# Attention probabilities transposed by VectorE blocks and SBUF-to-SBUF transfers instead of by TensorE

## Chip, core and metric

One core of a Trainium2 chip runs the whole program. The metric is the device time of one execution in microseconds (us); lower is better. Engines: PE is TensorE (PEld its weight loads), DVE VectorE, ACT ScalarE, POOL GpSimd, and SP issues all transfers here.

## What is computed

One layer of a generator over 1024 latent and 256 context tokens, width 1024, in float32. All tokens are normalised and projected; two branches follow, a gated linear attention (GLA) and a differential attention; gates merge them, and an output projection and a residual end the layer. The change lies in the differential attention: 8 heads, each with two sets of queries and keys of width 64 and one set of values of width 128.

```python
def diff_attention(q1, q2, k1, k2, v, lam):        # lq = 1024, keys = 1280
    def one_block(qs):                             # 128 queries
        qb1, qb2 = qs
        s1 = einsum('bhqd,bhkd->bhqk', qb1, k1) * scale
        s2 = einsum('bhqd,bhkd->bhqk', qb2, k2) * scale
        a = softmax(s1) - lam * softmax(s2)
        return einsum('bhqk,bhkv->bhqv', a, v)

o_diff = diff_attention(...)
b = merge_heads(rms_norm(o_diff) * diff_gain * (1 - lam_init)) * silu(diff_gate)
y = sigmoid(m_gla) * (a @ w_br_gla) + sigmoid(m_diff) * (b @ w_br_diff)
x = x + g_x * (y @ w_out)                          # g_x: a vector of the conditioning
```

## The kernel before

Full precision on PE is had by splitting: a float32 value becomes a rounded part `hi` and the difference `lo`, and a product is three matmuls (`mm3`: hi*hi, hi*lo, lo*hi). So whatever goes into such a product first needs a rounding and a subtraction.

The program runs in phases that overlap: projections (`phase_a`), GLA heads, differential attention with "filling" projections between its matmuls (`phase_b`, `fill`), and the branch and output projections (`phase_c`).

What sets the order of the work is a planner, class `Driver`. Each piece of the program is a Python generator that issues instructions and yields points in a planned time. The driver keeps a planned time for each engine, for the issue of transfers and for the tiles, by fixed costs, and resumes the generator with the best priority that is due. The result is one fixed order of instructions for each engine; on the chip each engine executes its own list in order and waits on semaphores. Buffers are counted: `acq(tag)` waits in the plan for a free buffer of a tag, `rel(tag, e)` gives one back; `TAGS` holds the number of each.

Attention goes over 8 heads and, in each, 8 query tiles `qt` of 128 queries; two tiles make a pair `pr`, so there are 64 tiles and 32 pairs. The steps of a tile:

- `att_scores`: PE writes both score rows (128 x 1280 each) into the PSUM tile `s5` (in profile rows `s`), 8 matmuls of 512 columns and 4 of 256. Queries `aq` and keys `kk` come from DRAM.
- `att_max`, `att_exp`: DVE takes the maxima (`sm<-s`), ACT the exponentials with their sums (`e<-s,sm`) into two `e5` tiles (rows `e`).
- `att_mix`: DVE combines both into one tile, `e<-e,sm,e`, 128 x 1280.
- `att_tr`: PE transposes the ten 128 x 128 blocks through PSUM (`b<-ident,e`; the last tiles `mc<-ident,e`), in groups of 4, 4 and 2 blocks (`GROUPS`).
- `att_split`, `split2`: ACT copies each group out of PSUM (`ac<-b`), POOL rounds it (`at<-ac`) and subtracts (`at<-ac,at`).
- `att_av`: for a pair, PE multiplies with the values, 30 matmuls of 256 columns (`b<-at,vv`).
- `att_fin`: two PE transposes of the result, squares on ACT, POOL's inverse root, a scaling on DVE (`b1k<-b1k,sm`), two PE transposes, a split, and a store to `d_bT`. Gates come from DRAM (`b1k<-d_dg`).

`fill` puts half tiles of other projections (24 matmuls of 512 columns, `mb<-h,wt`) on PE where the plan finds room, paced by `PACE`; its weights are loaded to `raw` and split to `wt` by ACT and DVE. `first_two` starts the product with `w_br_diff`, which needs `d_bT` of all heads back from DRAM (`h<-d_bT`). The gate vector `g_x`, halved, is computed once in `job_gate` as the tile `gb` and used in the last phase.

All engine instructions have the line of a helper: L190 for ACT, DVE and POOL, L326 for matmuls, L352 for PE transposes, L291 for transfers. So rows are read by tile names.

Of the kernel before, what the change touches and what calls it, by code (L numbers as in the profile page):

```python
# [221 lines left out]
class Hybrid:  # L222

    TAGS = dict(
        h0=("sb", 16), h1=("sb", 16), raw=("sb", 3), gb=("sb", 1), sm=("sb", 48), kk=("sbK", 3),
# [3 lines left out]
        hc=("sbA1", 16), g5=("sbA1", 6), l5=("sbA1", 3),  # L229
# [7 lines left out]
        e5=("sbB", 6), at4=("sbB", 6), at2=("sbB", 2), ac=("sbB", 2), b1k=("sbB", 5), fin=(None, 2),  # L237

        ya=("sbC", 8), yb=("sbC", 8), yc=("sbC", 8), yf=("sbC", 16), sf=("sbC", 2), o=("sbC", 4), wr=("sbC", 8),
# [141 lines left out]
    def scratch(self):  # L381
        d = self.dram
        self.d_q = [d(f"d_q{h}", [P, S]) for h in range(4)]
        self.d_k = [d(f"d_k{h}", [P, T]) for h in range(4)]
        self.d_la = [[d(f"d_la{r}{h}", [P, T]) for h in range(4)] for r in range(2)]
        self.d_v = [d(f"d_v{c}", [T, 512]) for c in range(2)]
        self.d_gg = [d(f"d_gg{c}", [S, 512]) for c in range(2)]
        self.d_dg = [d(f"d_dg{c}", [S, 512]) for c in range(2)]
        self.d_dv = [[d(f"d_dv{j}{c}", [T, 512]) for c in range(2)] for j in range(2)]
        self.d_qT = [d(f"d_qT{c}", [4, P, 2, S]) for c in range(2)]  # L390
        self.d_kT = [[d(f"d_kT{j}{c}", [4, P, T]) for c in range(2)] for j in range(2)]
        self.d_aT = [[d(f"d_aT{j}{h}", [2, P, S]) for h in range(4)] for j in range(2)]
        self.d_bT = [[d(f"d_bT{j}{i}", [P, S]) for i in range(8)] for j in range(2)]
        self.d_m = [[d(f"d_m{j}{i}", [P, S]) for i in range(8)] for j in range(2)]
        self.d_y = [d(f"d_y{i}", [P, S]) for i in range(8)]
# [333 lines left out]
    def job_gate(self):  # L729
# [4 lines left out]
        gb = self.gb = self.t("gb", [P, 2, 512])  # L734
        for n in range(2):
# [27 lines left out]
            self.rel("p", self.pool.tensor_scalar(gb[:, n], bias, 0.5, 0.0, ALU.mult, ALU.add))  # L763

# [29 lines left out]
    def phase_a(self):  # L794
# [6 lines left out]
        self.ev_rope = [Event(), Event()]  # L801
        self.ev_gla, self.ev_stream = Event(), Event()
# [57 lines left out]
    def to_gla(self):  # L860
        yield self.ev_la
        yield from self.idle("hc", "g5", "l5", "gs", "go", "gt")
# [638 lines left out]
    def att_mix(self, u):  # L1501
# [6 lines left out]
        if x in self.PC:  # L1508
            self.pool.tensor_scalar(E[1], E[1], cf, 0.0, ALU.mult, ALU.add)
            e = self.pool.tensor_tensor(E[0], E[0], E[1], ALU.add)  # L1510
# [4 lines left out]
        d.set(self.ev_a[u["hd"], u["qt"]], e)  # L1515
# [6 lines left out]
    def att_tr(self):  # L1522

        d = self.d
        for hd in range(8):
            for qt in range(8):
                x = qt % 2
                yield self.ev_a[hd, qt]
                E = self.att[hd, qt][0]
                if x == 0:  # L1530
                    A = self.aT[hd, qt // 2] = []
                for g, (k0, n) in enumerate(self.GROUPS):
                    if x == 0:
                        tg = "at4" if n == 4 else "at2"
                        yield from self.acq(tg, 2)
                        A.append([self.t(tg, [P, n, 2, P], F32R) for _ in range(2)] + [tg])
                    hi, lo = A[g][:2]
                    tb = "mc" if "psC" in self.pools else "b1"
                    yield from self.acq(tb)
                    pt = self.t(tb, [P, n, P])  # L1540
                    for j in range(n):
                        e = self.tr(pt[:, j], E[:, (k0 + j) * P:(k0 + j + 1) * P])
                    d.spawn(self.att_split(g, pt, hi[:, :, x], lo[:, :, x], self.ev_aT[hd, qt, g], tb), On(e, "ACT"), prio=self.PS)
                    yield AtPE(0)
                self.rel("e5", e)

    def att_av(self):
        d = self.d
        for hd in range(8):
            for pr in range(4):  # L1550
                for x in range(2):
                    yield self.ev_aT[hd, 2 * pr + x, 0]
                A = self.aT[hd, pr]
# [5 lines left out]
                for g, (k0, n) in enumerate(self.GROUPS):  # L1559
                    hi, lo, tg = A[g]  # L1560
                    for x in range(2):
                        yield self.ev_aT[hd, 2 * pr + x, g]
                    for j in range(n):
                        kt = k0 + j
                        e = self.mm3(po, VH[:, kt], VL[:, kt], hi[:, j].rearrange("p x t -> p (x t)"),
                                     lo[:, j].rearrange("p x t -> p (x t)"), kt == 0, kt == 9)
                        if j % 2:
                            yield AtPE(0)
                    self.rel(tg, e, 2)
                if pr == 3:  # L1570
                    self.rel("vv", e, 2)
                d.spawn(self.att_fin(hd, pr, po, [self.att[hd, 2 * pr + x][1] for x in range(2)]), On(e, "ACT"), prio=self.PF)
# [12 lines left out]
    def att_split(self, g, pt, hi, lo, ev, tag):  # L1585
        e = yield from self.split2(pt, hi, lo, tag, g in self.SG)
        self.d.set(ev, e)

    def split2(self, pt, hi, lo, tag, pool):

        yield from self.acq("ac")
        c = self.t("ac", [P, 4, P])[:, :pt.shape[1]]
# [13 lines left out]
    def att_fin(self, hd, pr, po, zs):  # L1606
# [7 lines left out]
        e = self.act.activation(ot, po, AF.Copy)  # L1614
# [23 lines left out]
        yield On(self.pool.tensor_tensor(ss, ss, self.nhalf[:, 0:2], ALU.pow), "DVE")  # L1638
        for x in range(2):
            e = self.dve.tensor_scalar(oo[:, x], g[:, x], ss[:, x:x + 1], None, ALU.mult)  # L1640
# [17 lines left out]
    def fill(self):  # L1658
# [17 lines left out]
        def conv(n, raw):  # L1676
# [6 lines left out]
            yield d.on("DVE", hi)  # L1683
            e = self.dve.tensor_tensor(lo, raw, hi.bitcast(F32), ALU.subtract)
# [100 lines left out]
    def first_two(self, evs, ws, rhs):  # L1785
# [3 lines left out]
        yield self.ev_aT[7, 7, 2]  # L1789
# [18 lines left out]
    def phase_b(self):  # L1808
# [22 lines left out]
        self.ev_aT = {(hd, qt, g): Event() for hd in range(8) for qt in range(8) for g in range(3)}  # L1831
        self.aT = {}
# [29 lines left out]
    def phase_c(self):  # L1862
# [6 lines left out]
        def to_c():  # L1869
# [6 lines left out]
            yield from self.idle("b1", "e5", "b1k", "aq", "kk", "vv", "at4", "at2", "ac")  # L1876
# [68 lines left out]
        def right():  # L1945

            w = {}

            def gate(n, k):
                x = w[n, k]  # L1950
                self.dve.tensor_tensor(x, x, self.gb[:, int(n[2]) - 1], ALU.mult)
# [148 lines left out]
```

## Time and profile before

| | before |
|---|---|
| three runs | 1717.92, 1720.37, 1720.63 us |
| median | 1720.37 us |
| span of the profiled execution, first to last instruction | 1714.5 us |
| busy PE, DVE, ACT, POOL | 1674.2, 1057.7, 738.3, 728.8 us |
| share of 16 DMA engines, moved | 48%, 258.8 MB |

The execution that was profiled has no time of its own besides its span; the span stands 5.9 us below the median of the runs. A profile row of a group reads: line, engine, operation, out<-in, shape, count | busy us, mean ns of one | idle us just before them, and what ended it. A row of the timeline reads: start us, us taken, engine, line, operation, tiles, count. The three numbers of a wait are us in total, times, and the longest.

### The profile page before, as it was taken

To read this page: it belongs to the slowest core of one execution; us is meant where nothing else is said; L and a number is where in the kernel's file an instruction comes from. 1 tells how busy PE (TensorE), PEld (TensorE's weight loads), DVE (VectorE), ACT (ScalarE), POOL (GpSimd) and SP (SyncE) were. 2 spreads that over 40 slices of the span, in tenths; PEclk is the share of its full clock that TensorE was granted. 3 is DMA by queue.
4 is the path that set the end of the run, shared out by engine and by line. 5 is a ranking of instruction groups with operands and counts; after the bars stand their busy time and mean duration, and the time that the engine had idled before them with its cause. 6 is when DMAs were issued, how large, how long until landed. Compare 5 with 4: busy or idle time off the path is not lost.

```text
span 1714.5 us, 24744 instructions
## 1 busy us (share of the span) xinstructions
PE 1674.2 (98%) x8557; PEld 1389.4 (81%) x8557; DVE 1057.7 (62%) x1933; ACT 738.3 (43%) x1509; POOL 728.8 (43%) x917
## 2 busy tenths in 40 slices
PE   8899999999999999999999989999999999999999
PEld 3788788888888888888888878888888888887887
DVE  4534325615564767767763788777877778325694
ACT  4636522212242443344342566656656556311231
POOL 1500002403324445444541577878878778710000
PEclk9999999999999999999999999999999999999999
DMA  8523344453743544535444244435436753269421
GB/s 309 158 86 122 143 154 149 140 171 115 221 163 114 202 142 147 168 125 168 160 129 143 91 119 137 117 108 145 133 105 185 226 156 114 84 238 333 148 98 74
DMA packets 244748, 258.81 MB, mean 151 GB/s; under 512 B 20840, under 2 KB 176400, under 8 KB 244624
## 3 DMA queue, kind: packets, MB, share of 16 engines
q1 hardware_dynamic: 244624, 257.25, 47.7%
q8 instruction: 67, 1.10, 0.3%
q14 instruction: 57, 0.47, 0.1%
HBM read 170.68 MB, written 86.51 MB: 150 GB/s over the span
## 4 chain that ended last, share of the span: by engine, by line
PE 87%; POOL 4%; DVE 2%; DMA 2%; ACT 2%; issue 2%; SPq 0%; ACTq 0%; DVEq 0%; POOLq 0%
PE mm L326 42%; PE mc L326 11%; PE mb L326 8%; PE s L326 7%; PE b L326 5%; POOL at L190 4%; PE b L352 3%; PE go L326 3%; PE gs L326 2%; PE gt L326 2%; PE tp L352 2%; DVE sm L190 1%; PE mz L326 1%; DMA w<-in_w_ada 1%; PE gt L352 1%
## 5 line engine op out<-in xcount | busy, mean ns | idle before, releaser
L326 PE MATMUL mm<-w,h 128*128 128x512 f32 x2304 | 569.3, 399 | 1.5 <-DVE w L190 1.5
L326 PEld LDWEIGHTS mm<-w,h 128*128 128x128 f32 x2304 | 425.6, 188 | 87.6 <-DVE w L190 2.1
L190 POOL TENSOR_TENSOR at<-ac,at 128x512 fp32r<-128x512 f32 (+1 forms) x192 | 239.6, 1248 | 16.0
L190 DVE TENSOR_REDUCE sm<-s 128x1 f32<-128x1024 f32 (+1 forms) x192 | 195.7, 1039 | 55.1 <-PE s L326 47.5
L326 PE MATMUL mb<-h,wt 128*128 128x512 f32 x720 | 200.2, 410 | 1.9 <-DVE ft L190 1.1
L190 ACT ACTIVATE e<-s,sm 128x1280 f32<-128x1280 f32 x128 | 170.0, 1331 | 49.3 <-DVE sm L190 41.5
L326 PE MATMUL s<-kk,aq 128*128 128x512 f32 (+1 forms) x768 | 180.5, 367 | 10.3 <-ACT e L190 3.2
L190 POOL TENSOR_SCALAR at<-ac 128x512 fp32r<-128x512 f32 (+1 forms) x192 | 139.2, 725 | 114.2 <-ACT ac L190 108.8
L190 ACT ACTIVATE ac<-b 128x512 f32<-128x512 f32 (+1 forms) x213 | 106.8, 507 | 141.9 <-PE b L352 103.5
L190 ACT ACTIVATE p<-mm 128x512 f32<-128x512 f32 (+1 forms) x116 | 67.6, 589 | 216.9 <-PE mm L326 198.5
L326 PEld LDWEIGHTS s<-kk,aq 128*128 128x128 f32 x768 | 122.2, 190 | 32.3 <-ACT e L190 12.6
L326 PEld LDWEIGHTS mb<-h,wt 128*128 128x128 f32 x720 | 127.7, 191 | 24.4 <-DVE ft L190 1.8
L326 PE MATMUL mc<-h,wt 128*128 128x512 f32 x624 | 144.1, 390 | 0.8 <-DVE wt L190 0.5
L326 PE MATMUL mm<-h,w 128*128 128x512 f32 x576 | 142.1, 399 | 2.3 <-ACT p L190 1.4
L190 POOL TENSOR_SCALAR sm<-sm 128x1 f32<-128x1 f32 (+1 forms) x78 | 16.8, 216 | 288.6 <-DVE sm L190 166.7
L326 PEld LDWEIGHTS mc<-h,wt 128*128 128x128 f32 x624 | 116.4, 188 | 25.4 <-DVE wt L190 1.0
L326 PE MATMUL b<-at,vv 128*128 128x256 f32 x960 | 132.1, 287 | 0.3
L326 PEld LDWEIGHTS b<-at,vv 128*128 128x128 f32 x960 | 123.5, 192 | 5.2 <-ACT ac L190 1.1
L326 PEld LDWEIGHTS mm<-h,w 128*128 128x128 f32 x576 | 107.1, 189 | 25.4 <-DVE h L190 1.7
L190 DVE TENSOR_TENSOR w<-raw,w 128x512 fp32r<-128x512 f32 x120 | 86.0, 734 | 63.5 <-ACT w L190 62.4
L190 POOL TENSOR_TENSOR sm<-sm,nhalf 128x1 f32<-128x1 f32 (+2 forms) x110 | 109.6, 997 | 10.4 <-DVE sm L190 3.9
L190 DVE SCALAR_TENSOR_TENSOR e<-e,sm,e 128x1280 f32<-128x1280 f32 x64 | 113.3, 1770 | 0.8
(225 smaller groups left out, 2358.6 us busy)
## 6 DMA issues: line engine op xcount, KB each, us to landing
raw<-in_w_in SPq DMA_DIRECT2D x72, 512.0 KB, 4.3
aq<-d_qT SPq DMA_DIRECT2D x128, 128.0 KB, 3.0
d_kT<-pl SPq DMA_DIRECT2D x40, 256.0 KB, 2.3
d_dv<-pl SPq DMA_DIRECT2D x40, 256.0 KB, 2.6
kk<-d_kT SPq DMA_DIRECT2D x32, 320.0 KB, 5.3
gv<-d_v SPq DMA_DIRECT2D x40, 256.0 KB, 2.8
vv<-d_dv SPq DMA_DIRECT2D x16, 640.0 KB, 6.3
d_aT<-gpl SPq DMA_DIRECT2D x64, 128.0 KB, 2.0
```

What stands on the lines that cost most here:

```text
L190: self.ins = f(out, *args, **kw).ins
L326: self.ins = self.nc.tensor.matmul(out, lhsT, rhs, start=start, stop=stop, skip_group_check=more).ins
L352: self.nc.tensor.transpose(out, src, self.ident[:n, :n])
```

## The change

A tile of combined probabilities is transposed in 32 x 32 blocks by one DVE instruction into a pair's tile `xt`, laid out so that what belongs to one 32-row strip of the result lies together. Then 16 transfers from SBUF to SBUF (32 partitions of 2560 bytes each, 80 KB) move each strip to its partitions in the tile `af`. ACT rounds `af` into `ah`, POOL subtracts in place, and `att_av` reads both in four pieces of 64 columns; `att_fin` undoes the order of columns in its copy out of PSUM.

With it: `e5` has 4 buffers for 6; `at4`, `at2` (6 and 2) are replaced by `xt` 2, `af` 2, `ah4` 3, `ah2` 2; `ac` has 1 for 2; `gb` is stored in DRAM and loaded again in the last phase. The scaling in `att_fin` moves from DVE to ACT, and the difference of the filling weights from DVE to POOL. The planner's costs stay, but its plan is made anew.

```diff
 # att_mix
-        if x in self.PC: ...
-        else:
-            e = self.dve.scalar_tensor_tensor(E[0], E[1], cf, E[0], ALU.mult, ALU.add)
-        self.att[u["hd"], u["qt"]] = (E[0], z)
+        e = self.dve.scalar_tensor_tensor(E[0], E[1], cf, E[0], ALU.mult, ALU.add)
+        self.rel("e5", e)
+        if x == 0:
+            yield from self.acq("xt")
+            self.X[hd, pr] = self.t("xt", [P, 4, 10, 2, 32])
...
+        yield d.on("DVE", E[0])
+        e = self.dve.transpose(X[:, :, :, x], E[0].rearrange("p (k c i) -> p c k i", c=4, i=32))
         self.rel("e5", e)
 # att_tr
-                    for j in range(n):
-                        e = self.tr(pt[:, j], E[:, (k0 + j) * P:(k0 + j + 1) * P])
-                    d.spawn(self.att_split(g, pt, hi[:, :, x], lo[:, :, x], ...), On(e, "ACT"), prio=self.PS)
+                yield from self.acq("af")
+                A = self.t("af", [P, 4, 10, 2, 32], F32R)
+                yield At(max(d.when(X), d.now) + 0.3)
+                for c in range(4):
+                    for r in range(4):
+                        e = self.dma(A[32 * c:32 * c + 32, r], X[32 * r:32 * r + 32, c])
+                self.rel("xt", e)
+                d.spawn(self.att_split(hd, pr, A), On(e, "ACT"), prio=self.PS)
+    def att_split(self, hd, pr, A):
+        for g, (k0, n) in enumerate(self.GROUPS):
+            tg = f"ah{n}"
+            yield from self.acq(tg)
+            h = self.t(tg, [P, 4, n, 2, 32], F32R)
...
+            yield On(self.act.activation(h, a.bitcast(F32), AF.Copy), "POOL")
+            e = self.pool.tensor_tensor(a, a.bitcast(F32), h.bitcast(F32), ALU.subtract)
 # att_av
+                    for kt in range(k0, k0 + n):
+                        m = [v.rearrange("p c x j -> p c (x j)") for v in (H[g][:, :, kt - k0], A[:, :, kt])]
+                        e = self.mm3(po, VH[:, kt], VL[:, kt], *m, kt == 0, kt == 9)
+                    self.rel(f"ah{n}", e)
+                self.rel("af", e)
 # att_fin
-            e = self.dve.tensor_scalar(oo[:, x], g[:, x], ss[:, x:x + 1], None, ALU.mult)
+            e = self.act.activation(oo[:, x], g[:, x], AF.Copy, scale=ss[:, x:x + 1])
 # fill, conv
-            e = self.dve.tensor_tensor(lo, raw, hi.bitcast(F32), ALU.subtract)
+            e = self.pool.tensor_tensor(lo, raw, hi.bitcast(F32), ALU.subtract)
 # job_gate; to_gla waits for ev_gb and for a free gb
+        self.store([(self.d_gb, gb)], ("gb", 1), ev=self.ev_gb)
 # phase_c, right
+            gb = self.t("gbc", [P, 2, 512])
+            self.dma(gb, self.d_gb)
```

The change moves instructions on every engine. PE's list in the third head, before: scores (`s`), then transposes of probabilities (`b<-ident,e`) among a filling projection (`mb`) and a transpose of `att_fin` (`b<-ident,b1k`).

```order
L326 MATMUL s_1828_8733<-kk_10011,aq_10237 128x512 x4
L352 MATMUL b_2275_10644<-ident,e_2157_10131 128x128 x2
L326 MATMUL mb_10540<-h_73_368,wt_10363 128x512
L326 MATMUL mb_10540<-h_74_369,wt_10363 128x512
L326 MATMUL mb_10540<-h_73_368,wt_10364 128x512
L352 MATMUL b_2277_10654<-ident,b1k_10633 128x128 x2
L352 MATMUL b_2282_10667<-ident,e_2175_10220 128x128 x4
```

The same engine after, where the product with the values of pair 12 (first of the fourth head) begins; `ah` and `af` are its rounded part and its difference, `vv` the values.

```order
L326 MATMUL mb_11381<-h_201_831,wt_10839 128x512
L326 MATMUL mb_11381<-h_202_832,wt_10839 128x512
L326 MATMUL mb_11381<-h_201_831,wt_10840 128x512
L326 MATMUL s_1828_8735<-kk_10562,aq_11208 128x512 x4
L326 MATMUL b_2365_11457<-ah_2319_11225,vv_10492 128x256
L326 MATMUL b_2365_11457<-af_11114,vv_10492 128x256
L326 MATMUL b_2365_11457<-ah_2319_11225,vv_11328 128x256
```

The transposes of `e` are gone from the list. Between a pair's last score and its first product with the values stand more filling matmuls than before: from the first to the last score of the program there are 816 for 696.

DVE at the first tiles of the fourth head, before: the combination, the scalings of `att_fin` (`b1k<-b1k,sm`), and the next maxima.

```order
L190 SCALAR_TENSOR_TENSOR e_2353_10985<-e_2355_10990,sm_11017,e_2353_10985 128x1280
L190 TENSOR_SCALAR sm_11083<-sm_10228 128x1
L190 TENSOR_SCALAR sm_11083<-sm_10309 128x1
L190 TENSOR_TENSOR b1k_11079<-b_2376_11098,b1k_11079 128x256
L190 TENSOR_SCALAR sm_11102<-sm_11102,sm_11083 128x1 x2
L190 TENSOR_SCALAR b1k_11101<-b1k_11079,sm_11102 128x128 x2
L190 TENSOR_REDUCE sm_11046<-s_1828_8733 128x1
```

And after, at the tiles of the same pair:

```order
L190 TENSOR_SCALAR sm_10928<-sm_10928,sm_10697,nlam 128x1
L190 STREAM_TRANSPOSE xt_10876<-e_2205_10628 128x40x32
L190 STREAM_TRANSPOSE xt_10876<-e_2213_10689 128x40x32
L190 SCALAR_TENSOR_TENSOR e_2238_10829<-e_2239_10832,sm_10928,e_2238_10829 128x1280
L190 STREAM_TRANSPOSE xt_10946<-e_2238_10829 128x40x32
L190 TENSOR_REDUCE sm_10912<-s_1828_8735 128x1
L190 RECIPROCAL sm_10960<-sm_10808 128x1
```

Each tile has gained a transpose. Both tiles of a pair stand here one behind the other, some 20 rows after their combinations, where the plan has a free `xt`; maxima of later tiles stand behind them.

SP's list, before, in the fourth head: stores of `att_fin` (`d_bT`), the gate of the next (`b1k<-d_dg`), queries, weights.

```order
L291 DMA d_bT_102<-b1k_11169 128x256
L291 DMA d_bT_110<-b1k_11170 128x256
L291 DMA b1k_11287<-d_dg_80 128x2x128
L291 DMA aq_11281<-d_qT_86 64x2x256 x2
L291 DMA aq_11284<-d_qT_86 64x2x256 x2
L291 DMA raw_11337<-in_w_in 128x8x128
L291 DMA d_m_125<-ft_11334 128x512
```

And after:

```order
L291 DMA aq_11035<-d_qT_87 64x2x256 x2
L291 DMA aq_11038<-d_qT_87 64x2x256 x2
L291 DMA raw_11106<-in_w_in 128x8x128
L291 DMA af_11114<-xt_10876 32x640 x16
L291 DMA d_bT_102<-b1k_11174 128x256
L291 DMA d_bT_110<-b1k_11175 128x256
L291 DMA d_m_126<-ft_11190 128x512
L291 DMA kk_11205<-d_kT_89 64x1280
```

Sixteen transfers of a pair stand together, ahead of the stores, keys and queries that follow.

More of the change, by code (lines that the diff above doesn't have):

```diff
@@ L733, in job_gate @@
         a = self.a
-        gb = self.gb = self.t("gb", [P, 2, 512])
+        yield from self.acq("gb")
+        gb = self.t("gb", [P, 2, 512])
         for n in range(2):
@@ L861, in to_gla @@
         yield self.ev_la
-        yield from self.idle("hc", "g5", "l5", "gs", "go", "gt")
+        yield self.ev_gb
+        yield from self.idle("gb", "hc", "g5", "l5", "gs", "go", "gt")
         self.close("sbA1")
@@ L1525, in att_tr @@
         for hd in range(8):
[L1526 to L1540, printed above, removed]
-                    for j in range(n):
-                        e = self.tr(pt[:, j], E[:, (k0 + j) * P:(k0 + j + 1) * P])
-                    d.spawn(self.att_split(g, pt, hi[:, :, x], lo[:, :, x], self.ev_aT[hd, qt, g], tb), On(e, "ACT"), prio=self.PS)
-                    yield AtPE(0)
-                self.rel("e5", e)
+            for pr in range(4):
+                for x in range(2):
+                    yield self.ev_a[hd, 2 * pr + x]
+                yield from self.acq("af")
+                X = self.X[hd, pr]
+                A = self.t("af", [P, 4, 10, 2, 32], F32R)
[6 more added lines that the diff above has]
+    def att_split(self, hd, pr, A):
+        self.aT[hd, pr] = (A, H := [])
+        for g, (k0, n) in enumerate(self.GROUPS):
+            tg = f"ah{n}"
+            yield from self.acq(tg)
+            h = self.t(tg, [P, 4, n, 2, 32], F32R)
+            H.append(h)
+            a, h = A[:, :, k0:k0 + n].rearrange("p c k x j -> p c (k x j)"), h.rearrange("p c k x j -> p c (k x j)")
+            yield On(self.act.activation(h, a.bitcast(F32), AF.Copy), "POOL")
+            e = self.pool.tensor_tensor(a, a.bitcast(F32), h.bitcast(F32), ALU.subtract)
+            self.d.set(self.ev_aT[hd, pr, g], e)
+            yield On(0, "ACT")
     def att_av(self):
@@ L1550, in att_av @@
             for pr in range(4):
-                for x in range(2):
-                    yield self.ev_aT[hd, 2 * pr + x, 0]
-                A = self.aT[hd, pr]
+                yield self.ev_aT[hd, pr, 0]
+                A, H = self.aT[hd, pr]
                 yield from self.acq("fin")
@@ L1682, in conv @@
             self.act.activation(hi, raw, AF.Copy)
-            yield d.on("DVE", hi)
-            e = self.dve.tensor_tensor(lo, raw, hi.bitcast(F32), ALU.subtract)
+            yield d.on("POOL", hi)
+            e = self.pool.tensor_tensor(lo, raw, hi.bitcast(F32), ALU.subtract)
             self.rel("raw", e)
@@ L1788, in first_two @@
         pms = []
-        yield self.ev_aT[7, 7, 2]
+        yield self.ev_aT[7, 3, 2]
         for x in range(4):
@@ L1830, in phase_b @@
         d.spawn(self.att_scores(), prio=0)
-        self.ev_aT = {(hd, qt, g): Event() for hd in range(8) for qt in range(8) for g in range(3)}
-        self.aT = {}
+        self.ev_aT = {(hd, pr, g): Event() for hd in range(8) for pr in range(4) for g in range(3)}
+        self.ev_x = {(hd, pr): Event() for hd in range(8) for pr in range(4)}
+        self.aT, self.X = {}, {}
         self.ev_u = [Event() for _ in range(64)]
@@ L1875, in to_c @@
             yield self.ev_att
-            yield from self.idle("b1", "e5", "b1k", "aq", "kk", "vv", "at4", "at2", "ac")
+            yield from self.idle("b1", "e5", "b1k", "aq", "kk", "vv", "xt", "af", "ah4", "ah2", "ac")
             self.close("psB1", "sbB2", "sbB", "sbK")
```

44 lines of the change are left out of this document (19 added, 25 removed).

## The prediction

> **What bounds the kernel now.** I read the page first: busy time of each engine, then the chain that ended last.
>
> ```profile
> span 1714.5 us, 24744 instructions
> ...
> PE 1674.2 (98%) x8557; PEld 1389.4 (81%) x8557; DVE 1057.7 (62%) x1933; ACT 738.3 (43%) x1509; POOL 728.8 (43%) x917
> ...
> PE 87%; POOL 4%; DVE 2%; DMA 2%; ACT 2%; issue 2%; SPq 0%; ACTq 0%; DVEq 0%; POOLq 0%
> ```
>
> PE works 98% of the span and is 87% of the chain. So an instruction taken off PE is worth its issue time, as long as PE stays the engine that is late. Where attention lies comes from the tile view of the queries: its score matmuls start from 938.0 to 1461.5 us (first row), the last ending at 1461.9. The stage table behind it shows the engines there and after.
>
> ```profile
> L326 PE MATMUL s<-kk,aq x768: 274/389/628, 938.0 to 1461.5; 128*128 128x512 f32 x128, 128*128 128x256 f32 x64
> ```
>
> ```profile
> core 0: us, PE busy (x) PEld busy (x) DVE busy (x) ACT busy (x) POOL busy (x), PEclk, DMA share, GB/s
> 937.00:1463.00 526.00, 506.61 (x3044) 432.94 (x3042) 405.16 (x723) 317.11 (x639) 407.27 (x437) 0.99 0.48 137
> 1463.00:1714.50 251.50, 244.52 (x1134) 203.73 (x1134) 137.64 (x220) 60.09 (x110) 35.87 (x43) 0.99 0.48 166
> ```
>
> In the score phase PE is busy 507 of 526 us, DVE 405, POOL 407, ACT 317. DVE idles 121 us there. The groups and waits of that window say what DVE does and what it waits for.
>
> ```profile
> L190 DVE TENSOR_REDUCE sm<-s 128x1 f32<-128x1024 f32 x191 | 194.5, 1038 | 55.1 <-PE s L326 47.5 <-ACT ac L190 2.6 <-ACT e L190 2.5
> L190 DVE SCALAR_TENSOR_TENSOR e<-e,sm,e 128x1280 f32<-128x1280 f32 x63 | 111.4, 1769 | 0.8
> L190 DVE TENSOR_SCALAR b1k<-b1k,sm 128x128 f32<-128x128 f32 x56 | 23.5, 463 | 36.0 <-POOL sm L190 35.9
> L190 DVE TENSOR_TENSOR wt<-raw,wt 128x1024 fp32r<-128x1024 f32 x14 | 21.3, 1518 | 0.0
> ```
>
> ```profile
> DVE sm L190 <- ACT e L190: 23.0, 16, 3.3
> ```
>
> **PE: what leaves.** 64 query tiles of 10 blocks are 640 transposes. The price is the slope of a run, since one alone overlaps its neighbours.
>
> ```profile
> 1146.44 0.60 PE L352 MATMUL b<-ident,e 128*128 128x128 f32 x4
> 1497.07 1.25 PE L352 MATMUL mc<-ident,e 128*128 128x128 f32 x10
> 1163.33 3.03 PE L326 MATMUL b<-at,vv 128*128 128x256 f32 x24
> 1149.38 0.96 PE L326 MATMUL b<-at,vv 128*128 128x256 f32 x6
> 1548.50 97.10 PE mc L326 x427
> ```
>
> (1.25 - 0.60) / 6 = 0.108 us, so 640 x 0.108 = 69 us leave PE. By the same slopes a 256-column matmul is 0.115 and a 512-column one 0.2275. With these I price PE's two orders. Before, from first to last score: 512 + 696 matmuls of 512 columns, 256 + 870 of 256, 704 transposes: 480 us, which took 523.9, so 44 were lost. After: 512 + 816, 256 + 816, 106: 437 us. (More of the filling projections now stand between the scores.) Behind the last score: before 241 us that took 252.6, so 11.5 lost; after 215.5. The AV matmuls now read their moving operand in four pieces of 64 columns; no row shows that form. A gain is excluded, since as many columns go through. The nearest row, 64-column matmuls of the linear attention, has 32.0 / 256 = 0.125 us each; against 0.115 that would be 10 us on 960. I take nothing, by the 256-column row, and keep 10 for the range.
>
> ```profile
> L326 PE MATMUL gs<-gqr,gkk 128*128 128x64 f32 x256 | 32.0, 268 | 0.0
> ```
>
> **DVE: what comes.** 64 block transposes of 128x1280. No row has this operation. The nearest: the product over the same 1280 elements takes 1.77 us here and 1.49 where POOL is quiet; above it stands the scan (0.477 for 128, so at most 4.8 for 1280), below it the scaling by a column (0.786 for 1024, so 0.98).
>
> ```profile
> L190 DVE SCALAR_TENSOR_TENSOR g<-g,g 128x1280 f32<-128x1280 f32 x8 | 11.9, 1492 | 0.2
> L190 DVE TENSOR_TENSOR_SCAN gla<-ones,gla 128x128 f32<-128x128 f32 x80 | 34.5, 477 | 2.8 <-DMA gla<-d_la 2.8
> L190 DVE TENSOR_SCALAR g<-g,sm 128x1024 f32<-128x1024 f32 x10 | 7.9, 786 | 14.8 <-POOL sm L190 14.8
> ```
>
> So one transpose costs T between 0.98 and 4.8; I take 1.6, between the two prices of the same 1280 elements. DVE loses the b1k scaling (23.5) and the wt difference (21.3). DVE in the score phase: 405.2 - 44.8 + 64 x 1.6 = 463 us, against PE's 437. DVE becomes the late engine. Of its 121 us of idle, the wait for POOL's rsqrt goes (35.9, that scaling now runs on ACT), and so does most of the wait for PE's scores (47.5), since PE is now early; 37 stay (the exponentials' sums 23, and smaller ones). Score phase: 463 + 37 = 500 us.
>
> The transposes also bring a wait: they need a free `xt`, given back when the transfers of two pairs before have landed. Behind a transpose that waits stand the next tile's maxima on DVE; ACT's exponentials wait for those, and PE's next scores for the exponentials. An `xt` is held for a tile's DVE work (7.2 us), the issue of 16 transfers (8 to 10, below) and a landing (3.1): 20 of the 31 us that two tiles allow. So nothing on the sum; at more than 31 it would be the loop that sets the pace.
>
> The Trainium skill, page "VectorE: DVE Perf Modes", section "Rules for kernel authors", says the opposite of this change: a 128x128 transpose belongs on TensorE if PSUM will do as its destination. Its section "The three transpose paths" gives 311 ns on VectorE for 128x128 bf16. Ten such would be 3.1 us a tile, an estimate from that page; with it the sum below would be 1773 instead of 1677. Its 390 ns for TensorE is not what the run above shows (0.108 each, back to back); what VectorE takes, no row of this trace shows.
>
> **ACT and POOL.** ACT drops 192 copies out of PSUM and gains 96 roundings (64 of 1024 elements, 32 of 512) and 64 scalings. POOL drops its roundings, keeps the differences in pieces twice as large, and gains the weights' differences.
>
> ```profile
> L190 POOL TENSOR_TENSOR at<-ac,at 128x512 fp32r<-128x512 f32 (+1 forms) x192 | 239.6, 1248 | 16.0
> L190 POOL TENSOR_SCALAR at<-ac 128x512 fp32r<-128x512 f32 (+1 forms) x192 | 139.2, 725 | 114.2 <-ACT ac L190 108.8
> L190 ACT ACTIVATE ac<-b 128x512 f32<-128x512 f32 (+1 forms) x213 | 106.8, 507 | 141.9 <-PE b L352 103.5
> L190 ACT ACTIVATE wt<-raw 128x1024 fp32r<-128x1024 f32 x28 | 29.6, 1064 | 68.1 <-PE mc L326 49.0 <-DMA h<-d_bT 15.3 <-issue 3.9
> L190 ACT ACTIVATE b1k<-b 128x128 f32<-128x128 f32 (+1 forms) x96 | 29.5, 314 | 27.4 <-PE b L326 17.0 <-PE b L352 10.1
> 1160.26 1.29 POOL L190 TENSOR_TENSOR at<-ac,at 128x512 fp32r<-128x512 f32 x1
> 1146.70 0.73 POOL L190 TENSOR_TENSOR at<-ac,at 128x256 fp32r<-128x256 f32 x1
> ```
>
> ACT: -192 x 0.51 + 64 x 1.06 + 32 x 0.51 + 64 x 0.31 = +6 us. POOL: -139; the differences at 2.41 for 1024 (slope of 1.29 and 0.73) and 1.29 for 512 are 195 instead of 240; 28 weight differences add 67: -117 in all. Both stay under 70% of the phase, so on the sum I put nothing; a POOL late by one 2.41 us piece is hidden, because PE's order has 24 us of work between a pair's scores and its AV at the start and 40 to 66 later.
>
> **SP.** Each of 32 pairs adds 16 transfers of 80 KB, 41.9 MB in all. Nearest rows: seven narrow loads one behind the other, and the 64-partition query loads; then, from the DMA view, the us to landing (last column).
>
> ```profile
> 57.67 3.56 SPq L291 DMA_DIRECT2D l<-in_gla_w_decay  x7
> 1306.12 2.46 SPq L291 DMA_DIRECT2D aq<-d_qT  x4
> ```
>
> ```profile
> aq<-d_qT SPq DMA_DIRECT2D x120, 128.0 KB, 3.1
> ```
>
> ```profile
> d_bT<-b1k SPq DMA_DIRECT2D x64, 128.0 KB, 2.4
> ...
> h<-d_bT SPq DMA_DIRECT2D x32, 256.0 KB, 5.4
> ...
> l<-in_gla_w_decay SPq DMA_DIRECT2D x8, 32.0 KB, 5.1
> ```
>
> 3.56 / 7 = 0.51 and 2.46 / 4 = 0.62 a transfer: 8 to 10 us a pair. SP already issues 332 transfers from 937 to 1480 us, which at 0.5 are 5.2 us a pair. So SP needs 13 to 15 us of a pair's 15.6 (500 / 32). It is in order: behind a group that waits for DVE's transposes or for a free `af` (given back by PE's AV two pairs before) stand the next query loads, gate loads and the stores of bT, and PE and DVE wait for the first two. Cover: queries are loaded two pairs ahead. I put nothing on the sum, and the bad end into a rival. DMA's share of 0.48 at 137 GB/s becomes 0.77 by bytes (84 GB/s more); the transfers' landing is inside the 24 us above: 8.2 + 3.1 + 1.06 + 2.41 = 15.
>
> The gate vector gb makes a round trip through DRAM: one store in the projection phase, where the linear attention starts much later, and one load while PE still has some 100 us of other matmuls before it needs a gated weight: nothing; without that cover one landing of 5.4 us. At the end, PE has only 9.5 us of work between the last AV and the first matmul that needs head 7's bT, and that chain takes about 15 (a store of 2.4, a load of 5.4, and some 7 for two pairs of PE transposes and the ACT, DVE and POOL steps between): 6 us on the path, which before lay under projections that are now done earlier.
>
> **The sum.** 938 + 500 + (215.5 + 11.5 + 6) = 1671 us of span. The execution shown spans 1714.5 and the median run is 1720.4, so 5.9 lie around it: 1677 us.
>
> **Rivals.** (a) PE stays the bound. For it: DVE at 463 of 480 would just fit. Against: 37 us of DVE's waits have causes that the change leaves. Score phase 437 + 44 lost as before: 938 + 481 + 233 = 1652, 1658 us.
>
> (b) SP is the bound, and the gain is lost there. At 0.62 a transfer SP issues 15.1 us a pair, 483 us. If the in-order wait at the head of each group costs 1.8 us, the phase is 541 and the time 938 + 541 + 233 + 5.9 = 1718: no change. For it: 15.1 of 15.6 us leaves no room for any wait. Against: at 0.51 SP has 2 us a pair to spare, and the loads behind it are asked for two pairs ahead.
>
> The Trainium skill, page "DMA: Bandwidth & Descriptors", section "Rules for kernel authors", advises against transfers to separate groups of partitions, since all use the same engines and serialize. The seven loads above follow one another every 0.51 us while each lands after some 5 us, so they overlap in this trace.
>
> (c) Slower: the block transpose of 4-byte data takes two passes, T = 2.98 (twice the quiet 1.49). DVE is then 360 + 191 + 37 = 588 us, and the time 938 + 588 + 233 + 5.9 = 1765. The point from which the change loses: 543.5 - 37 - 360.4 = 146 us for 64, T = 2.28. For it: no row shows a 4-byte transpose; against: the other rows over 1280 4-byte elements go in one pass at 1.49.
>
> **How the numbers follow.** DVE bound with T from 1.4 to 2.0: 0.42, 1664 to 1703. PE bound: 0.22, 1640 to 1664 (below 1658 if the 44 lost shrink, since some of them were PSUM waits of the transposes). SP: 0.19, 1700 to 1745, half of it a gain. Slow transpose: 0.14, 1725 up to 1881 (T = 4.8). The rest, 0.03, on the slow side. A 0.2% band (3.4 us, what this measurement can tell) round 1720 gets 0.05. Faster: 0.42 + 0.22 + 0.08 = 0.72; slower 0.23. The range cuts off the far part of (c) and a little of (a): 1645 to 1740.
>
> **What would show it.** Right: transposes of 1.5 to 1.8 us on DVE, DVE over 85% busy between first and last score, that phase near 500 us, PE's busy share down and its idle time put on DVE or on ACT behind DVE. Wrong: a transpose over 2.28; PE still over 96% busy there (rival a); query or gate loads landing late, with SP never idle (rival b). AV matmuls with a slope above 0.115 would add to the time by their own.

## The result, and the profile after

The changed kernel takes 1842.99 us (median of 4 runs, 1836.18 to 1846.46), the kernel before 1719.23 in runs on the same chip: a ratio of 1.072, 95% interval 1.0692 to 1.0747. It is slower by 7%; 1677 was forecast. The execution profiled spans 1844.7 us. From its page, the spans and engines, and the chain that ended last:

```profile
span 1844.7 us, 23960 instructions
...
PE 1654.8 (90%) x7917; PEld 1359.6 (74%) x7917; DVE 1098.3 (60%) x1905; ACT 746.7 (40%) x1477; POOL 634.4 (34%) x657
...
PE 17%; SPq 11%; DMA 10%; issue 2%; ACT 1%; DVE 1%; POOL 1%; ACTq 0%; DVEq 0%; POOLq 0%
```

PE was 87% of the chain. Now the part of the chain that could be followed is shared with SP's queue and with DMA. Next, PE's score matmuls by the tile view of the queries (durations ns, first and last start), and the stage table:

```profile
L326 PE MATMUL s<-kk,aq x768: 274/393/796, 937.8 to 1587.1; 128*128 128x512 f32 x128, 128*128 128x256 f32 x64
```

```profile
core 0: us, PE busy (x) PEld busy (x) DVE busy (x) ACT busy (x) POOL busy (x), PEclk, DMA share, GB/s
937.00:1593.00 656.00, 507.23 (x2531) 421.32 (x2530) 455.90 (x715) 323.98 (x597) 287.69 (x181) 0.89 0.65 172
1593.00:1844.70 251.70, 223.39 (x1006) 184.46 (x1006) 129.90 (x202) 61.72 (x120) 55.94 (x38) 0.94 0.54 173
```

The score phase grew from 523.5 to 649.3 us: 126 of the 130 us by which the two spans differ. No compute engine fills it: PE idles 149 of 656 us, DVE 200, ACT and POOL more. SP's rows in the timeline show what does (start, us taken, transfers in a row); behind them stands the chain's share by line in 1100 to 1300 us, and what DVE waited for in the score phase (total, times, longest).

```profile
1171.10 11.06 SPq L291 DMA_DIRECT2D af<-xt  x16
1182.22 0.58 SPq L291 DMA_DIRECT2D b1k<-d_dg  x1
1182.91 0.43 SPq L291 DMA_DIRECT2D d_m<-ft  x1
1183.39 0.43 SPq L291 DMA_DIRECT2D b1k<-d_dg  x1
1183.98 10.01 SPq L291 DMA_DIRECT2D af<-xt  x16
1194.10 2.50 SPq L291 DMA_DIRECT2D aq<-d_qT  x4
```

```profile
by line: SPq L291 36.9%; PE s L326 12.9%; PE mb L326 11.6%; DMA vv<-d_dv 8.2%; PE b L326 8.1%; issue 5.8%; ACT e L190 3.3%; DMA aq<-d_qT 3.1%; DMA af<-xt 3.1%; DVE sm L190 1.4%; DMA b1k<-d_dg 1.2%; POOL af L190 1.2%; PE b L352 0.9%; DVE xt 
```

```profile
DVE sm L190 <- PE s L326: 75.2, 52, 11.3
DVE xt L190 <- DMA af<-xt: 51.9, 13, 10.9
DVE sm L190 <- ACT e L190: 27.7, 22, 3.5
DVE b1k L190 <- DMA b1k<-d_dg: 27.4, 6, 10.6
```

```profile
PE s L326 <- ACT e L190: 88.1, 35, 9.6
```

Most groups of 16 take SP 10 to 12 us. Here two groups stand back to back: the gate load `b1k` gets through between them, the queries only after 23 us. Meanwhile `xt` isn't given back, DVE's next transpose waits for it (51.9 us, longest 10.9), and behind that wait the maxima, the exponentials and the scores: the last line has PE's own wait for the exponentials, 88.1 us, where it was 3.2 before. For the query loads themselves the score matmuls waited 0.7 us in the whole run, so those still came in time. SP's waits in 937 to 1593 add up to 157 us (before, in 937 to 1463: 358). What is left of the window counts here as SP's work: 499 of 656 us, 15.6 a pair.

### The profile page after: what moved, and what is told of

Read it like the earlier page. It is cut to its first block, busy times and chain, and to the rows that moved or that the text cites. A ratio compares the mean times of both kernels' runs of the same rounds, so it can differ in the third digit from the quotient of the medians.

```text
span 1844.7 us, 23960 instructions
## 1 busy us (share of the span) xinstructions
PE 1654.8 (90%) x7917; PEld 1359.6 (74%) x7917; DVE 1098.3 (60%) x1905; ACT 746.7 (40%) x1477; POOL 634.4 (34%) x657
## 5 line engine op out<-in xcount | busy, mean ns | idle before, releaser
L190 POOL TENSOR_TENSOR af<-af,ah 128x1024 fp32r<-128x1024 f32 (+1 forms) x96 | 205.3, 2151 | 260.9 <-ACT ah L190 163.6
L326 PE MATMUL s<-kk,aq 128*128 128x512 f32 (+1 forms) x768 | 197.8, 397 | 100.1 <-ACT e L190 88.1
L326 PE MATMUL mb<-h,wt 128*128 128x512 f32 x840 | 222.6, 412 | 24.9 <-ACT ft L190 19.0
L326 PEld LDWEIGHTS mb<-h,wt 128*128 128x128 f32 x840 | 163.6, 200 | 62.5 <-ACT ft L190 21.3
L190 ACT ACTIVATE ah<-af 128x1024 fp32r<-128x1024 f32 (+1 forms) x96 | 85.1, 910 | 166.1 <-DMA af<-xt 155.7
L326 PE MATMUL b<-ah,vv 128*128 128x256 f32 x640 | 136.9, 299 | 3.4 <-ACT ah L190 2.9
L190 DVE STREAM_TRANSPOSE xt<-e 128x1280 f32<-128x1280 f32 x64 | 95.7, 1503 | 64.3 <-DMA af<-xt 59.4
L326 PE MATMUL mc<-h,wt 128*128 128x512 f32 x504 | 120.5, 399 | 8.6 <-DMA h<-d_bT 7.3
L326 PEld LDWEIGHTS b<-ah,vv 128*128 128x128 f32 x640 | 113.5, 207 | 7.0 <-ACT ah L190 3.3
L326 PEld LDWEIGHTS mc<-h,wt 128*128 128x128 f32 x504 | 96.2, 193 | 29.3 <-DMA h<-d_bT 7.7
L190 POOL TENSOR_TENSOR wt<-raw,wt 128x1024 fp32r<-128x1024 f32 x28 | 74.5, 2662 | 119.6 <-ACT wt L190 112.6
```

The lines of the kernel that those rows point to most:

```text
L190: self.ins = f(out, *args, **kw).ins
L326: self.ins = self.nc.tensor.matmul(out, lhsT, rhs, start=start, stop=stop, skip_group_check=more).ins
```

## The experiments

Ratios are against the kernel before on the same chip. "Same order" means that the instruction lists of PE, DVE, ACT and POOL are word for word those of the kernel named.

### Is it SP's issues, or the bytes, or the rest of the change?

```diff
 # four (one: a single transfer of A <- X); the planner is still told of 16
-                for c in range(4):
-                    for r in range(4):
-                        e = self.dma(A[32 * c:32 * c + 32, r], X[32 * r:32 * r + 32, c])
+                for r in range(4):
+                    self.nc.sync.dma_start(A[:, r].bitcast(F32), X[:, r])
```

> The changed kernel with 4 transfers a pair in place of 16: each carries one quarter of xt's columns of all 128 partitions to the same partitions of af, so the bytes, the buffers and the waits are the same and only the number of issues falls. The move across partitions is left out, so the output is another. The planner is told of 16 transfers as before, and the order of instructions on PE, DVE, ACT and POOL is unchanged word for word. Theory S (SP's issue time, 16 x 0.63 = 10.1 us a pair, in order with all loads and stores): SP loses 12 x 0.63 = 7.6 us a pair, 242 us in all, so the score phase falls from 649 to 510-540 us and the time from 1843 to 1700-1735. Rival B (bytes and landing times of the transfers, DMA share 0.65): the bytes are the same, so within 1% of 1843. Rival O (the static order, the buffers, or the other edits on POOL and ACT): order and buffers are the same, so above 1800.

> As the kernel with 4 transfers a pair, but with one of 128 partitions x 10 KB; the move across partitions is left out again, the bytes and the order of the engines' work are unchanged. Theory S: a further 3 x 0.6 = 1.9 us a pair leaves SP, which is no longer late: 1690-1730, at most 1% under the kernel with 4. Rival B: within 1% of 1843. Rival O: above 1800. If one issue takes as long as its bytes (0.6 us for 80 KB, so 9 to 10 us for 1.3 MB), the issue time is one by bytes and not by count, and both kernels stay above 1800.

1725.45 us (1.0039, 1.0027 to 1.0051) with four, 1723.51 (1.0028, 1.0015 to 1.0041) with one: 117 to 119 us come back when the number of issues falls, with bytes, buffers and order kept. The tile view of `af` gives the time of an issue (ns, min/median/max): changed kernel, four, one.

```profile
L291 SPq DMA_DIRECT2D af<-xt x512: 507/588/4683, 959.7 to 1646.0; - x171
```

```profile
L1547 SPq DMA_DIRECT2D af<-xt x128: 470/602/4848, 963.2 to 1528.3; - x128
```

```profile
L1546 SPq DMA_DIRECT2D af<-xt x32: 471/506/4195, 959.5 to 1518.7; - x32
```

80, 320 and 1280 KB take SP 0.59, 0.60 and 0.51 us: it pays for the instruction, not for the bytes. Is the cost a line or a threshold?

```diff
+                [self.nc.sync.dma_start(A[64 * h:64 * h + 64, r].bitcast(F32), X[64 * h:64 * h + 64, r])
+                 for r in range(4) for h in range(2)]
```

> As the kernel with 4 transfers a pair, the order of PE, DVE, ACT and POOL the same word for word, but with 8 of 64 partitions, the same bytes in all (the move across partitions left out). SP has 8 x 0.6 = 4.8 us a pair for them beside some 5.2 of other issues, in a pair's 17. If each issue costs the same, the time lies on the line between 1725 (4) and 1843 (16): 1764. If it is a queue that costs little until it is nearly full, as theory S has it: 1728-1750.

1749.04 us (1.0173, 1.0153 to 1.0192). For 1, 4, 8 and 16 issues a pair: 1723.5, 1725.5, 1749, 1843. The first three added cost 2 us, the next four 24, the last eight 94: each issue costs more the fuller the queue is, and the measured 1749 lies at the upper end of theory S's range. Two things change together with the number. The transfers grow wider as they become fewer (32, 64, then 128 partitions) and no longer cross partitions; sixteen of the wide form were not tried. But an issue takes as long at each of these widths (0.59, 0.60 and 0.60 us), and the DMA engines are no busier with 16 (0.65 of the phase) than with four (0.67). And the move itself becomes shorter, from some 12 us (10 of issue and 2.1 of landing) to 6 with four (2.5 and 3.5). The next two kernels, made from the kernel before, tell that apart from the delay of other loads.

### SP's load alone, on the kernel before

```diff
 # att_tr of the kernel before, at the second tile of a pair
+                if x: dd = self.t("dd", [P, 4, 640])
+                      (16 x) nc.sync.dma_start(dd[32 * c:32 * c + 32, r], E[32 * r:32 * r + 32, 0:640])
 # the second kernel reads self.V[hd][0] (values, long loaded) in place of E
```

> The kernel before, with nothing taken from it, and 16 transfers a pair added on SP: 32 partitions x 640 columns of the second mixed tile of a pair to a tile that nothing reads. The planner isn't told, and the order on PE, DVE, ACT and POOL is that of the kernel before. Theory S: SP's 350 us of waits in the score phase take most of 323 us, but loads queue behind groups of 10 us: the loss is seen without DVE's transposes and without the exchange being waited for, 1770-1850. If the loss needs the work that waits for the transfers (the chain transposes, transfers, split, AV and the release of xt, Rival L), a tile that nobody reads costs little: 1720-1745.

> The kernel before with 16 transfers a pair added on SP (0.63 us each), as in the kernel that gave 1832, but read from the values' tile, which is long loaded and is kept to the end of a head: no engine waits for these transfers, and they wait for nothing. Theory S1 (the other loads and stores come late behind them in SP's one row): still 1790-1830. Theory S2 (the loss there was the 83 us that exponentials waited for the transfers to release the tile): 1720-1750.

1832.03 (1.0661, 1.0643 to 1.0678) and 1783.47 (1.037, 1.0354 to 1.0385), both in the same order as before. With nothing else of the change, 16 transfers a pair cost 113 us where engines wait for the tile they read, and 65 where nobody waits for them. The waits say which way (first the kernel that reads `e`, then the one that reads the values):

```profile
ACT e L190 <- DMA dd<-e: 82.9, 17, 11.9
```

```profile
DVE b1k L190 <- DMA b1k<-d_dg: 43.9, 11, 11.1
PEld b L352 <- DVE b1k L190: 38.5, 14, 10.9
```

In the first, ACT can't reuse `e` until the late group has read it. In the second the gate loads stand behind the groups (43.9 us of waits, before 4.8 in the whole phase), and PE's transposes in `att_fin` behind DVE. So both theories hold for a part, the late loads of S1 for up to 65 of the 113 us and the release of S2 for the other 48, and the 1783 lies outside both ranges. The transfers also bring 42 MB of bytes; as many bytes cost 25 us in a later run with two issues a pair, so the queue alone may be some 40 of the 65, an estimate.

### Another queue

```diff
-                        e = self.dma(A[...], X[...])
+                        e = self.dma(A[...], X[...], q=self.nc.gpsimd)                       # all 16 on POOL
+                        e = self.dma(A[...], X[...], q=self.nc.scalar if r % 2 else None)    # 8 on ACT, 8 on SP
```

> The changed kernel, whole, with its 16 transfers a pair issued by POOL and not by SP; POOL does the split behind them in any case and works 9 us of a pair's 20. What an issue costs on POOL no run has shown yet. Theory S: SP is as free as before; at 0.6 us an issue POOL works 19 us a pair and the time is 1740-1800; at 0.3 us or less 1715-1740; at 1.0 us or more POOL is the new bound with 25 us a pair and the time is 1900 or more. Rival (the transfers themselves and not SP): 1840 or more with POOL having idle time.

> The changed kernel, whole, with 8 of a pair's 16 transfers issued by ACT and 8 by SP; the planner isn't told. Theory S (issue time, each queue its own): SP keeps 5 of 10 us a pair; ACT's work grows from 10.1 to 15.1 us of a pair's 17-20, and its exponentials stand behind issues that wait for the transposes: between 1740 and 1830. If the issue time is shared by both queues, so that one engine's issue waits for the other's, 1840 or more. If ACT's issues are nearly free to ACT (0.1 us or less), 1720-1750.

1909.13 (1.1104, 1.1085 to 1.1123) and 1888.6 (1.1002, 1.0976 to 1.1028): both worse than 16 on SP. POOL's issues as a group in the first; then, in the second, ACT's and SP's issues by the tile view and one of ACT's waits:

```profile
L291 POOL DMA_DIRECT2D af<-xt x512 | 254.2, 503 | 88.0 <-DMA af<-xt 42.9 <-DVE xt L190 26.9 <-issue 10.0
```

```profile
L291 ACTq DMA_DIRECT2D af<-xt x256: 513/601/1757, 960.4 to 1685.1; - x128
L291 SPq DMA_DIRECT2D af<-xt x256: 507/588/3273, 960.8 to 1685.4; - x128
```

```profile
ACT e L190 <- DMA af<-xt: 133.8, 19, 12.6
```

An issue takes ACT 0.60 us and POOL 0.50. SP's own takes 0.59 beside ACT's, as it did alone: the two don't slow each other's issues. So the rival of a shared issue time is out, and yet the time is 1889, since ACT's exponentials wait 134 us behind the transfers in ACT's own row. My price for half on ACT (1740 to 1830) had that row in it and made it too small. At 0.5 us an issue POOL should have come out under 1800 by theory S; it too waits in its row, 88 us ahead of these issues, and the splits and inverse roots stand behind them.

### What keeps few issues at 1725, and not at the forecast 1677?

```diff
 # no mix, in the kernel with one transfer          # transposes added to the kernel before
-        e = self.dve.scalar_tensor_tensor(E[0], E[1], cf, E[0], ALU.mult, ALU.add)
+        self.nc.vector.transpose(dd[:, :, :, x], E[0].rearrange("p (k c i) -> p c k i", c=4, i=32))
```

> The kernel with one transfer a pair, and the mix of the two exponentials on DVE (64 instructions of 1.77 us, 113 us) left out, so the output is another; the planner still counts them, so the order on the other engines is unchanged. Question: with SP relieved, why is the score phase 545 us and not the forecast 500? Theory D (DVE in order: a maximum waits behind a transpose and a mix, ACT behind the maximum, PE behind the exponential, since each score tile has one buffer): the phase falls to 470-495 us and the time to 1650-1675. Rival C (PE itself, by its lower granted clock of 0.95 in the phase and its order): the phase stays over 530 and the time over 1705.

> The kernel before, with nothing taken from it, and DVE's 64 block transposes added (1.5 us each, 96 us) into a tile that nobody reads. Theory D: DVE's 405 us become 501 in a phase of 529, and with DVE in order its waits don't shrink to 28 us: the phase grows by 20-50 us, 1740-1770. Rival: DVE has 120 us to spare in the phase, so the transposes fit: 1720-1728.

1708.98 (0.995, 0.9931 to 0.9968) and 1755.24 (1.0207, 1.0192 to 1.0222). Added to the kernel before, 96 us of DVE work cost 36: its idle time was to spare only in part, as theory D had it. But 113 us taken from DVE in the kernel with one transfer gave back 15, where theory D said 48 or more. The stage table and the chain's share (1100 to 1300 us) of that run:

```profile
937.00:1463.00 526.00, 464.90 (x2461) 391.02 (x2460) 339.87 (x631) 312.95 (x580) 252.07 (x176) 0.95 0.70 212
```

```profile
by line: PE mb L327 26.6%; PE s L327 18.7%; PE b L327 16.7%; DMA af<-xt 16.0%; ACT e L190 4.2%; DVE sm L190 3.8%; DVE xt L190 3.2%; issue 2.9%; DMA kk<-d_kT 2.6%; PE b L353 1.6%; DMA aq<-d_qT 1.3%; ACT wt L190 1.0%; SPq L292 0.7%; ACT ft L1
```

DVE is busy 340 of 526 us and not late, so theory D falls for this kernel. The time is in rival C's range, but PE idles 61 us here, so a clock of 0.95 alone can't be it; on the chain stands the landing of the transfer, 16%. So the third theory, M: the moving itself. A kernel in which the move is free:

```diff
-                yield from self.acq("af")
-                A = self.t("af", [P, 4, 10, 2, 32], F32R)
-                (16 transfers)
+                A = X
 # att_split: hi and lo in tiles of their own (ah4 has 4, ah2 has 2), xt given back after the last difference
+            h, l = [self.t(tg, [P, 4, n, 2, 32], F32R) for _ in range(2)]
```

> The changed kernel with a move that costs nothing: no transfers, no af; the split reads xt where it lies and writes both halves to tiles of their own (four of 512 and two of 256 columns a partition, which fit where af stood), so xt comes free at the split and not after a transfer. The move across partitions is left out and the output is another. The planner plans anew. DVE has its 96 us of transposes, PE is without its 69 us. Theory M (all of the loss is in the moving: SP's issues, 122 us, and then the landing and the buffers held for it, 45 us): the score phase is 495-515 us, as was forecast, and the time 1670-1700. Theory D (DVE's longer work is what keeps the kernel with one transfer at 1723): 1710-1730 again.

1668.9 us (0.9719, 0.9704 to 0.9733), faster than the kernel before by 2.8%. Its score rows, stage table and chain share in 1100 to 1300:

```profile
L326 PE MATMUL s<-kk,aq x768: 274/389/797, 939.7 to 1429.4; 128*128 128x512 f32 x128, 128*128 128x256 f32 x64
```

```profile
937.00:1434.00 497.00, 460.44 (x2538) 388.61 (x2537) 475.41 (x725) 329.20 (x624) 309.76 (x193) 0.99 0.53 149
1434.00:1667.50 233.50, 224.16 (x1009) 183.49 (x1007) 127.95 (x192) 53.82 (x93) 46.49 (x26) 1.00 0.52 173
```

```profile
by line: DVE sm L190 23.7%; DVE e L190 14.8%; issue 14.7%; PE mb L326 13.2%; PE s L326 12.5%; PE b L326 8.1%; POOL ah L190 4.7%; DVE xt L190 3.8%; DVE b1k L190 1.1%; ACT e L190 1.0%; POOL b1k L190 0.9%; PE b L352 0.9%; POOL sm L190 0.3%; AC
```

The score phase is 490 us, DVE is busy 475 of 497 and leads the chain. So the forecast's compute side came true, and the loss lies in the moving. What of it is not SP's issues:

```diff
 # replan4: four transfers, and the planner told of four
+                for r in range(4):
+                    e = self.dma(A[:, r]..., X[:, r]...)
 # bytes: the free move, and 1.3 MB a pair that nobody reads
+                [self.nc.sync.dma_start(dd[:, n], V) for n in range(2)]
 # early: replan4 with one af, split into tiles of their own as in the free move
+            if g == 2: self.rel("af", e)
```

> The kernel with 4 transfers a pair (the move across partitions left out), but the planner is told of 4 and not of 16, and lays out the order of PE, DVE, ACT and POOL anew. Theory O (the order, laid out for 16 transfers, is what keeps it at 1725): 1685-1705. Theory M (the landing and xt, af and e5 held for it): 1715-1735. The planner's price of an issue, 0.45 against 0.63 measured, is of no weight if the two kernels agree within 0.5%.

> The kernel with the free move (1669 us; the move across partitions left out), with the bytes of the move added: two transfers a pair on SP from the values' tile, 640 KB each, to a tile that nobody reads. Rival B (42 MB more in the phase delay the other loads): 1695 or more, and landings of the queries, keys and values are longer. Theory H (the hold of the buffers, not the bytes): 1668-1685.

> 4 transfers a pair of 128 partitions from xt to af (the move across partitions left out), as in the kernel that gave 1735, but the split writes both halves to tiles of their own, so af comes free at the split and not at the end of AV; one af in place of two, to make room for them. The planner plans anew. Theory H: 1680-1705, near the free move. Rival L (two more waits in the chain from the mix to AV, landing 3.5 us): 1715 or more.

1735.4 (1.0112, 1.0092 to 1.0132), 1693.88 (0.986, 0.9839 to 0.9881) and 1710.98 (0.9954, 0.9938 to 0.9969). A plan that knows of four is 10 us slower than the plan for 16, so theory O is out, and an order made anew moves the time by some 10 us of itself. Bytes that nobody waits for, with their two issues, cost 25 us; that they do so through late landings of other loads isn't seen, since those landings stayed within 0.6 us of the free move's. What is seen is that PE takes 1618 us for the same 7917 matmuls that take 1608 in the free move, at a granted clock of 0.96 for 0.99 in the phase; whether that is the way was not tried. Waiting for the transfers adds 17, and holding `af` to the end of AV another 24. The last two times, 1694 and 1711, fall between the ranges of their theories. The three kernels have orders of their own, so these are sizes to some 10 us each; together they are 66 us, and 57 if the kernel with four in the changed kernel's order is taken for the last.

### Whole versions

```diff
 # by DRAM: 4 stores that lay the blocks down in their new order, 1 load; split in place as in the changed kernel
+                for r in range(4):
+                    e = self.dma(W[:, r].rearrange("(c i) e -> i c e", c=4), X[32 * r:32 * r + 32]...)
+                e = self.dma(A..., W)
 # early16: the 16 transfers with the early release
 # by DRAM, early: each tile's xt is stored at once, 4 loads, early release
+            e = self.dma(W[x], X.rearrange("p c k j -> p (c k j)"))
+                    e = self.dma(A[32 * c:32 * c + 32]..., W[c])
 # buffers: the kernel before with
-        e5=("sbB", 6)
+        e5=("sbB", 4)
```

> The whole computation, with the exchange by way of DRAM: 4 stores of 32 partitions x 10 KB that lay the blocks down in their new order, then one load of 128 partitions x 10 KB: 5 issues a pair in place of 16, twice the bytes and a second landing. The planner is told and plans anew. Theory S: SP loses 11 x 0.63 = 6.9 us a pair: 1700-1760. Rival B (bytes): 84 MB where there were 42, so slower than 1843. Rival L (the time from the last transpose to the split): some 4 us more a pair, 1843 or more.

> The whole computation with 16 transfers a pair and the early release of af (one af, tiles of their own for both halves of the split). Theory S (SP's issue time): the 10 us a pair stay, 1780-1845. If early release covers SP's groups: under 1760.

> The whole computation, by way of DRAM with 6 issues a pair and early release: each transposed tile (its own xt, three of them) is stored at once by one transfer of 128 partitions x 5 KB, and four loads of 32 partitions fetch the blocks in their new order to af; the split writes tiles of its own, and the products come out in query order. SP has 6 x 0.63 = 3.8 us a pair. Theories S and H together: 1690-1740. Rival B (84 MB, as in the kernel by DRAM that gave 1787): 1760 or more.

> The kernel before with 4 buffers of e5 and not 6, as in the changed kernel, and nothing else: the planner lays out its order for 4. What the buffers alone cost: nothing to 10 us (1716-1730) if the buffers of the mixed tiles don't matter, as the prediction took it; 1735 or more if they are a second cause of the loss.

1787.07 (1.04, 1.0378 to 1.0421), 1829.89 (1.0654, 1.0632 to 1.0676), 1774.08 (1.0326, 1.0299 to 1.0354) and 1714.19 (0.9979, 0.9968 to 0.999). With 16 issues the early release saves 13 us, so SP stays the cause. Five or six issues by way of DRAM win back 56 and 69 us and stay slower than before. In the better one the DMA engines are busy for 0.93 of 937 to 1520 us, and the gate loads land later (last column of the DMA view, us from issue to landing; second row the changed kernel).

```profile
b1k<-d_dg SPq DMA_DIRECT2D x32, 128.0 KB, 7.3
```

```profile
b1k<-d_dg SPq DMA_DIRECT2D x32, 128.0 KB, 3.1
```

I left its bytes out of the price (1690 to 1740 for S and H together, and 1700 to 1760 for the first); rival B's 1760 or more came true. Of all whole versions only the kernel before with four `e5` beats both, by 0.2%. Even the unreal one with four transfers and early release is 0.5% under the kernel before, so I followed the change no further.

## Why the prediction was wrong

- **SP: the step that failed.** "13 to 15 us of a pair's 15.6 ... I put nothing on the sum", with the cover "queries are loaded two pairs ahead". The count was right: 5.25 us of other issues ((526 - 358) / 32 before), 0.63 an issue, 15.6 us a pair. The cover held for what it names, as the scores waited 0.7 us for query loads. It did not cover the rest of the row: the transfers themselves, with them the release of `xt` (51.9 us of DVE's waits), and the gates (27.4, before 4.8). With issues cut to four or one the same kernel is 118 us faster; with 16 added the kernel before is 113 us slower.
- **Rival (b) named the mechanism and mis-sized it.** It gave SP 1.8 us of waits a pair and 1718 us. Measured: 15.6 of work and 4.9 of waits (157 / 32), 20.5 us, the 656 us of the window. But few of these waits are the ones that it named, at the head of a group for transposes or for a free `af`: for transposes SP waits 5.2 us in the whole window, and 25.4 for PE to be done with a buffer, such as `af`. That is at most 1 us a pair where it took 1.8; the others stand elsewhere in the row, such as 26.3 for `att_fin`'s results to store. Of its sign, "query or gate loads landing late, with SP never idle", DVE's waits for gates alone were seen.

```profile
SPq L291 <- POOL b1k L190: 26.3, 18, 4.9
SPq L291 <- PE b L326: 25.4, 10, 7.5
SPq L291 <- DVE xt L190: 5.2, 2, 3.9
```

- **"20 of the 31 us that two tiles allow. So nothing on the sum".** Mis-sized: 57 us (1725.5 against 1668.9) even where SP has room. It is bytes, the wait for the landing and the hold of `af` to the end of AV; the first and the last I had not priced. How it divides is only known to some 10 us.
- **T = 1.6 was right:** 1.50.

```profile
L190 DVE STREAM_TRANSPOSE xt<-e 128x1280 f32<-128x1280 f32 x64 | 95.7, 1503 | 64.3 <-DMA af<-xt 59.4
```

Rival (c) is out with it. The Trainium skill, page "VectorE: DVE Perf Modes", section "The three transpose paths", gives 311 ns for 128x128 bf16, and ten of those would be 3.1 us a tile, an estimate; the trace doesn't agree, 1.50 for float32. The advice of its section "Rules for kernel authors" to transpose 128 x 128 on TensorE holds here all the same, for another reason: the blocks have to be moved afterwards.
- **PE, DVE and the sum came out where the move is free:** phase 500 forecast, 490 measured; behind the last score 233 forecast, 238; 1677 forecast, 1669. "DVE becomes the late engine" is seen there, and rival (a) isn't. That the sum came so near is in part luck: DVE worked 471 us of the phase for 463 and idled 19 for 37, and this kernel has an order of its own, with 725 filling matmuls between the scores and not 816. AV in four pieces keeps its slope: by two runs of the chain of the kernel with the free move, (2.14 - 1.44) / 6 = 0.117 against 0.115.

```profile
1109.38 2.14 PE b L326 x18
1128.13 1.44 PE b L326 x12
```

- **The landing of a transfer** (3.1 taken) is 2.1 us, not a loss. The granted clock is 0.89 in the changed kernel's phase, where PE idles 149 of 656 us, and 0.99 in the free move's, where it idles 37 of 497; PE takes 1655 us in all for the matmuls that take 1608 there. So up to 46 of the 174 us between the two kernels pass through a slower PE. Whether idle time, the added bytes or something else lowers the clock was not tried.
- **Not tried apart:** the side moves to ACT and POOL and the trip of `gb` through DRAM. They are in the kernel with the free move, which came out 8 us under the forecast; four `e5` alone cost nothing.

The Trainium skill, page "DMA: Bandwidth & Descriptors", section "Issuing engines are not separate DMA queues", calls the time that an engine takes to start a transfer usually small beside the transfer. By this trace it is 0.59 of a 2.1 us landing, paid in order and 16 times, and it decides. The same page's advice in "Rules for kernel authors", one transfer of 128 partitions in place of two to disjoint halves, fits the runs with eight, four and one; its reason, that such transfers share the same engines, is not what these runs show, since the DMA engines were not full (0.65 of the phase with 16).

## What to carry to other kernels

Price the issuing queue as an engine: transfers times the time of an issue, however small the bytes, plus the waits of a row kept in order. By the window less SP's waits, SP at work for 52% of the score phase (four issues a pair) cost 2 us more than at 41% (one); at 61% (eight) it cost 24 us over four, at 76% (sixteen) 118. "Loaded ahead" covers the loads and nothing else, since releases go through the same row. A cheaper way to compute something isn't cheaper until the data is where the next step wants it; a run with the move left out shows in one step what there is to win (2.8% here).

## What of the hardware was unexpected

- An issue takes the same time on SP for 80 KB and for 320 KB (0.59 and 0.60 us), less for 1280 KB in one (0.51), and the same on ACT (0.60); POOL takes 0.50.
- A block transpose of 128 x 1280 float32 takes DVE 1.50 us, no longer than a product over as many elements (1.49).
